# Small inputs first on another queue, a split first load, and two stores on the loads' queue in a rotary-embedding kernel

## The chip, the cores and the metric

One core of one Trainium2 chip. The metric is the device time of one execution in microseconds (us); a profile's span is about 1.8 us shorter, since it runs only from the first to the last instruction. All runs compared here are of the fast state, unless it is said otherwise. Most runs of a kernel lie within 0.3% of its median. A transfer is "asked for" when an engine issues it and "lands" when its semaphore reports the whole of it. Units, casts and stores are counted from 0 in the order of work, loads X1 to X7 by their unit.

## The reference, cut to what matters

```python
# x: (8, 8, 1024, 64) fp32, 16.78 MB; freqs: 32 fp32; positions: 1024 integers
angles = np.outer(positions * scale, freqs)
cos, sin = np.cos(angles), np.sin(angles)
x_first, x_second = x[..., :half], x[..., half:]
out_first  = x_first * cos - x_second * sin
out_second = x_first * sin + x_second * cos
```

All of x is read once and all of the output, as large, is written once. The sine and cosine tables depend on positions and freqs alone and are the same for every head.

## The kernel before

x is cut into eight units of 2 MiB (128 partitions, 16 KiB each). Unit 0 comes as fp32 from SyncE and is cast by ScalarE. Units 1 to 7 are cast to fp16 by the transfer itself, issued from GpSimd. VectorE does four fp16 passes a unit, 6.93 us in all; ScalarE casts the result into one of four fp32 OUT buffers, which is stored from SyncE. The first of the four passes writes the tile ps. Before the first unit stands the table chain: positions and freqs, two small matmuls, four passes on VectorE, two sines on ScalarE.

```python
BUF_O = 4
...
    X0f = xin.tile([P, N], FP32, name="X0f")
    nc.sync.dma_start(out=X0f, in_=xv[0])

    pos_i64 = consts.tile([HP, K], positions.dtype)
    nc.scalar.dma_start(out=pos_i64, in_=positions.rearrange("(q k) -> q k", k=K))
    freq_row = consts.tile([1, half], FP32)
    nc.scalar.dma_start(out=freq_row, in_=freqs[None, :])
    ...
    load(1)                    # nc.gpsimd.dma_start(X[1], fp32 -> fp16)
    ...                        # two GpSimd instructions build sel
    for u in range(2, NU):
        load(u)
    ...                        # tables: cfreq, pos_ps, y, m, r, sinT, ra, cosT
    for u in (1, 0, *range(2, NU)):
        ps = prods.tile([P, K, 2, half], FP16, tag="ps")
        ...                    # four VectorE instructions on X[u] and ps
        OUT = xout.tile([P, N], FP32, tag="O")
        pin(nc.scalar.copy(out=OUT, in_=X[u].rearrange("p k h j -> p (k h j)")))
        nc.sync.dma_start(out=ov[u], in_=OUT)
```

Of the kernel before, what the change touches and what calls it, by code (L numbers as in the profile page):

```python
# [1 line left out]

# [1 line left out]

# [4 lines left out]

FP32 = mybir.dt.float32
FP16 = mybir.dt.float16
I32 = mybir.dt.int32
AF = mybir.ActivationFunctionType
ALU = mybir.AluOpType

_MAGIC = 12582912.0
_TWO_PI_DN = float(np.float32(np.uint32(0x40C90FDA).view(np.float32)))

BUF_O = 4  # L20
BUF_P = 2


@with_exitstack
def kernel(
    ctx: ExitStack,
    tc: tile.TileContext,
    x: bass.AP,
    freqs: bass.AP,
    positions: bass.AP,  # L30
    scale: bass.AP,
    out: bass.AP,
):
    nc = tc.nc

    B, Hh, S, D = x.shape
    NBH = B * Hh
    half = D // 2
    P = nc.NUM_PARTITIONS
    HEADS = 8  # L40
    HP = P // HEADS
    K = S // HP
    N = K * D
    NU = NBH // HEADS
    assert S % HP == 0 and D == 2 * half and NBH % HEADS == 0

    fscale = float(scale)

    xv = x.rearrange("b h s d -> (b h s d)").rearrange("(u p n) -> u p n", p=P, n=N)
    ov = out.rearrange("b h s d -> (b h s d)").rearrange("(u p n) -> u p n", p=P, n=N)  # L50

    consts = ctx.enter_context(tc.tile_pool(name="consts", bufs=1))
    tmp = ctx.enter_context(tc.tile_pool(name="tmp", bufs=1))
    psum = ctx.enter_context(tc.tile_pool(name="psum", bufs=1, space=bass.MemoryType.PSUM))
    xin = ctx.enter_context(tc.tile_pool(name="xin", bufs=1))
    xout = ctx.enter_context(tc.tile_pool(name="xout", bufs=BUF_O))
    prods = ctx.enter_context(tc.tile_pool(name="prods", bufs=BUF_P))


    X0f = xin.tile([P, N], FP32, name="X0f")  # L60
    nc.sync.dma_start(out=X0f, in_=xv[0])

    pos_i64 = consts.tile([HP, K], positions.dtype)
    nc.scalar.dma_start(out=pos_i64, in_=positions.rearrange("(q k) -> q k", k=K))  # L64
    freq_row = consts.tile([1, half], FP32)
    nc.scalar.dma_start(out=freq_row, in_=freqs[None, :])

    X = [xin.tile([P, K, 2, half], FP16, name=f"X{u}") for u in range(NU)]

    def load(u):  # L70
        nc.gpsimd.dma_start(out=X[u].rearrange("p k h j -> p (k h j)"), in_=xv[u])  # L71


    sel = consts.tile([HP, HEADS, HP], FP32)
    load(1)
    nc.gpsimd.memset(sel, 0.0)
    nc.gpsimd.affine_select(  # L77
        out=sel, in_=sel, compare_op=ALU.not_equal, fill=1.0, base=0,
        pattern=[[0, HEADS], [-1, HP]], channel_multiplier=1,
    )  # L80
    for u in range(2, NU):
        load(u)

    pin = tc.keep_in_program_order


    coef = consts.tile([1, P], FP32)
    pin(nc.vector.memset(coef, fscale / (2.0 * np.pi)))  # L88
    quarter = consts.tile([P, 1], FP32)
    pin(nc.vector.memset(quarter, np.pi / 2.0))  # L90
    cfreq = psum.tile([P, half], FP32)
    nc.tensor.matmul(out=cfreq, lhsT=coef, rhs=freq_row, start=True, stop=True)  # L92

    pos_row = consts.tile([HP, K], FP32)
    pin(nc.vector.tensor_copy(  # L95
        out=pos_row,
        in_=pos_i64.bitcast(I32).rearrange("p (k t) -> p k t", t=2)[:, :, 0],
    ))
    pos_ps = psum.tile([P, K], FP32)
    nc.tensor.matmul(  # L100
        out=pos_ps, lhsT=sel.rearrange("q a b -> q (a b)"), rhs=pos_row, start=True, stop=True
    )
    posf = consts.tile([P, K], FP32)
    pin(nc.vector.tensor_copy(out=posf, in_=pos_ps))  # L104

    y = tmp.tile([P, K, half], FP32)
    pin(nc.vector.tensor_tensor(  # L107
        out=y,
        in0=posf.unsqueeze(2).broadcast_to((P, K, half)),
        in1=cfreq.unsqueeze(1).broadcast_to((P, K, half)),  # L110
        op=ALU.mult,
    ))
    m = tmp.tile([P, K, half], FP32)
    pin(nc.vector.tensor_scalar(out=m, in0=y, scalar1=_MAGIC, scalar2=None, op0=ALU.add))  # L114
    r = tmp.tile([P, K, half], FP32)
    pin(nc.vector.scalar_tensor_tensor(  # L116
        out=r, in0=m, scalar=_MAGIC, in1=y, op0=ALU.subtract, op1=ALU.subtract
    ))
    sinT = consts.tile([P, K, half], FP16)
    pin(nc.scalar.activation(out=sinT, in_=r, func=AF.Sin, bias=0.0, scale=-_TWO_PI_DN))  # L120
    ra = tmp.tile([P, K, half], FP32)
    pin(nc.vector.tensor_scalar(  # L122
        out=ra.bitcast(I32), in0=r.bitcast(I32), scalar1=0x7FFFFFFF, scalar2=None, op0=ALU.bitwise_and
    ))
    cosT = consts.tile([P, K, half], FP16)
    pin(nc.scalar.activation(out=cosT, in_=ra, func=AF.Sin, bias=quarter, scale=-_TWO_PI_DN))  # L126
    pin(nc.scalar.copy(out=X[0].rearrange("p k h j -> p (k h j)"), in_=X0f))  # L127

    cos_b = cosT.unsqueeze(2).broadcast_to((P, K, 2, half))
    sin_b = sinT.unsqueeze(2).broadcast_to((P, K, 2, half))  # L130


    for u in (1, 0, *range(2, NU)):
        ps = prods.tile([P, K, 2, half], FP16, tag="ps")
        pin(nc.vector.tensor_tensor(out=ps, in0=X[u], in1=sin_b, op=ALU.mult))  # L135
        pin(nc.vector.tensor_tensor(out=X[u], in0=X[u], in1=cos_b, op=ALU.mult))  # L136
        pin(nc.vector.tensor_tensor(  # L137
            out=X[u][:, :, 0, :], in0=X[u][:, :, 0, :], in1=ps[:, :, 1, :], op=ALU.subtract
        ))
        pin(nc.vector.tensor_tensor(  # L140
            out=X[u][:, :, 1, :], in0=ps[:, :, 0, :], in1=X[u][:, :, 1, :], op=ALU.add
        ))
        OUT = xout.tile([P, N], FP32, tag="O")
        pin(nc.scalar.copy(out=OUT, in_=X[u].rearrange("p k h j -> p (k h j)")))  # L144
        nc.sync.dma_start(out=ov[u], in_=OUT)


# [1 line left out]
_INS = ['x', 'freqs', 'positions', 'scale']  # L149
_OUTS = [((8, 8, 1024, 64), 'float32')]  # L150

_NUMBERS = {'scale': 0.5}


# [26 lines left out]
```

## Time and profile before

| | before |
|---|---|
| median time, 3 runs | 85.48 us (85.28 to 85.62) |
| span | 83.9 us |
| VectorE busy | 62.6 us, from 9 to 73 with no gap over 0.7 us |
| DMA engines | full from about 4 us to 82 us |
| bytes | 16.79 MB read, 16.78 MB written |

The prediction below shows the main lines. Two more views matter for what came of it. The first is the page's list of transfers: what, from which queue, KB each, us from issue to landing.

```profile
X0f<-in_x_dram SPq DMA_DIRECT2D x1, 2048.0 KB, 10.2
pos_i<-in_positions_dram ACTq DMA_DIRECT2D x1, 8.0 KB, 4.1
```

Positions, 8 KB, are 4.1 us on the way beside unit 0. The second is the table by stretches at the end; its last two columns are the busy share of the DMA engines and the GB/s moved.

```profile
76.00:77.00 1.00, 0.00 (x0) 0.00 (x0) 0.00 (x0) 0.41 (x1) 0.00 (x0) 1.00 0.62 262
```

Just as the last store is asked for (76.43), the DMA engines have a small dent. They had almost run out of stores at the moment when the last one came. By the semaphore record of the trace it landed at 82.68, 6.25 us after it was asked for. The experiments below show that this is what a store takes with no other store ahead of it.

### The profile page before, as it was taken

The numbers are of one execution on the slowest core, as the hardware profiler recorded it, in microseconds if no ns is written. First come the engines' busy times: TensorE is split into PE (matmuls) and PEld (weight loads), VectorE is DVE, ScalarE is ACT, GpSimd is POOL, SyncE is SP. The second block draws the span as 40 slices with busy tenths as digits, with TensorE's granted clock in tenths as the row PEclk, the third lists the DMA queues.
The fourth block names the chain that finished last, engine by engine and source line by source line (L and its number), as shares of the span: only waits on it lengthen the run. The fifth ranks groups of instructions, "written<-read, shape, count | busy, mean of one in ns | idle before, by whom it ended". The sixth has DMA issues, their size and how long they took to land.

```text
span 83.9 us, 151 instructions
## 1 busy us (share of the span) xinstructions
PE 1.1 (1%) x4; PEld 0.9 (1%) x4; DVE 62.6 (75%) x40; ACT 37.4 (45%) x12; POOL 4.5 (5%) x13
## 2 busy tenths in 40 slices
PE   0002300000000000000000000000000000000000
PEld 0002200000000000000000000000000000000000
DVE  0010699889999999999999999999999999600000
ACT  1400000799749309608905921950880591294000
POOL 5960000000000000000000000000000000000000
DMA  3599999999999999999999999999999999998890
GB/s 78 207 402 328 289 207 219 215 211 223 203 230 203 231 191 238 313 336 305 313 348 324 313 313 277 426 438 438 438 430 414 445 414 430 438 430 375 375 500 0
DMA packets 2338, 26.22 MB, mean 313 GB/s; under 512 B 274, under 2 KB 290, under 8 KB 290
## 3 DMA queue, kind: packets, MB, share of 16 engines
q1 hardware_dynamic: 1296, 18.87, 53.6%
q0 software_dynamic: 1008, 7.34, 42.7%
q10 hardware_dynamic: 34, 0.01, 0.2%
HBM read 16.79 MB, written 16.78 MB: 400 GB/s over the span
## 4 chain that ended last, share of the span: by engine, by line
DVE 72%; DMA 8%; ACT 7%; DVEq 1%; PE 1%; issue 1%; ACTq 1%
DVE X L136 22%; DVE ps L135 21%; DVE X L137 12%; DVE X L140 9%; DMA freq_row<-in_freqs_dram 8%; ACT OUT L144 4%; DVE r L116 3%; DVE y L107 3%; ACT sinT L120 2%; DVE m L114 1%; DVEq L176 1%; PE cfreq L92 1%; PE pos_ps L100 1%; ACTq L64 0%; DVE posf L104 0%
## 5 line engine op out<-in xcount | busy, mean ns | idle before, releaser
L144 ACT CAST OUT<-X 128x4096 f32<-128x4096 f16 x8 | 28.8, 3605 | 25.0 <-DVE X L140 25.0
L135 DVE TENSOR_TENSOR ps<-X,sinT 128x4096 f16<-128x4096 f16 x8 | 18.3, 2284 | 0.7 <-ACT sinT L120 0.7
L136 DVE TENSOR_TENSOR X<-X,cosT 128x4096 f16<-128x4096 f16 x8 | 18.3, 2292 | 0.3
L137 DVE TENSOR_TENSOR X<-X,ps 128x2048 f16<-128x2048 f16 x8 | 9.8, 1224 | 0.3
L140 DVE TENSOR_TENSOR X<-ps,X 128x2048 f16<-128x2048 f16 x8 | 9.7, 1217 | 0.0
L120 ACT ACTIVATE sinT<-r 128x2048 f16<-128x2048 f32 x1 | 1.9, 1910 | 12.2 <-DVE r L116 12.2
L71 POOL DMA_DIRECT2D X<-in_x_dram x7 | 3.9, 567 | 0.8 <-POOLq L162 0.8
L127 ACT CAST X<-X0f 128x4096 f16<-128x4096 f32 x1 | 3.6, 3587 | 0.0
L104 DVE COPY posf<-pos_ps 128x64 f32<-128x64 f32 x1 | 0.2, 225 | 4.0 <-PE pos_ps L100 4.0
L95 DVE CAST pos_row<-pos_i 16x64 f32<-16x64 int32 x1 | 0.2, 241 | 3.9 <-DMA pos_i<-in_positions_dram 3.9
L116 DVE SCALAR_TENSOR_TENSOR r<-m,y 128x2048 f32<-128x2048 f32 x1 | 2.3, 2292 | 0.0
L107 DVE TENSOR_TENSOR y<-posf,cfreq 128x2048 f32<-128x2048 f32 x1 | 2.3, 2286 | 0.0
L120 ACT ACT_TABLE_LOAD x1 | 1.3, 1283 | 1.7 <-issue 1.7
L126 ACT ACTIVATE cosT<-ra,quarter 128x2048 f16<-128x2048 f32 x1 | 2.0, 1985 | 0.0
L114 DVE TENSOR_SCALAR m<-y 128x2048 f32<-128x2048 f32 x1 | 1.2, 1227 | 0.0
L122 DVE TENSOR_SCALAR ra<-r 128x2048 int32<-128x2048 int32 x1 | 1.2, 1226 | 0.0
L88 DVE MEMSET coef<- 1x128 f32 x1 | 0.2, 165 | 0.8 <-PEq L162 0.8
L92 PE MATMUL cfreq<-freq_row,coef 1*128 1x32 f32 x2 | 0.6, 392 | 8.0 <-DMA freq_row<-in_freqs_dram 8.0
L100 PE MATMUL pos_ps<-pos_row,sel 16*128 16x64 f32 x2 | 0.7, 432 | 0.0
L92 PEld LDWEIGHTS cfreq<-freq_row,coef 1*128 1x128 f32 x2 | 0.5, 308 | 7.9 <-issue 7.9
L100 PEld LDWEIGHTS pos_ps<-pos_row,sel 16*128 16x128 f32 x2 | 0.5, 328 | 0.0
L77 POOL TENSOR_SCALAR_AFFINE_SELECT sel<-sel 16x128 f32<-16x128 f32 x1 | 0.3, 332 | 0.1
(6 smaller groups left out, 0.7 us busy)
## 6 DMA issues: line engine op xcount, KB each, us to landing
out_dram<-OUT SPq DMA_DIRECT2D x8, 2048.0 KB, 14.3
X<-in_x_dram POOLq DMA_DIRECT2D x7, 1024.0 KB, 24.5
X0f<-in_x_dram SPq DMA_DIRECT2D x1, 2048.0 KB, 10.2
pos_i<-in_positions_dram ACTq DMA_DIRECT2D x1, 8.0 KB, 4.1
freq_row<-in_freqs_dram ACTq DMA_DIRECT2D x1, 0.1 KB
```

Source lines behind the costliest of these rows:

```text
L71: nc.gpsimd.dma_start(out=X[u].rearrange("p k h j -> p (k h j)"), in_=xv[u])
L100: nc.tensor.matmul(out=pos_ps, lhsT=sel.rearrange("q a b -> q (a b)"), rhs=pos_row, start=True, stop=True)
L107: pin(nc.vector.tensor_tensor(out=y, in0=posf.unsqueeze(2).broadcast_to((P, K, half)), in1=cfreq.unsqueeze(1).broadcast_to((P, K, half)), ...
L114: pin(nc.vector.tensor_scalar(out=m, in0=y, scalar1=_MAGIC, scalar2=None, op0=ALU.add))
L116: pin(nc.vector.scalar_tensor_tensor(out=r, in0=m, scalar=_MAGIC, in1=y, op0=ALU.subtract, op1=ALU.subtract))
L120: pin(nc.scalar.activation(out=sinT, in_=r, func=AF.Sin, bias=0.0, scale=-_TWO_PI_DN))
L127: pin(nc.scalar.copy(out=X[0].rearrange("p k h j -> p (k h j)"), in_=X0f))
L135: pin(nc.vector.tensor_tensor(out=ps, in0=X[u], in1=sin_b, op=ALU.mult))
L136: pin(nc.vector.tensor_tensor(out=X[u], in0=X[u], in1=cos_b, op=ALU.mult))
L137: pin(nc.vector.tensor_tensor(out=X[u][:, :, 0, :], in0=X[u][:, :, 0, :], in1=ps[:, :, 1, :], op=ALU.subtract))
L140: pin(nc.vector.tensor_tensor(out=X[u][:, :, 1, :], in0=ps[:, :, 0, :], in1=X[u][:, :, 1, :], op=ALU.add))
L144: pin(nc.scalar.copy(out=OUT, in_=X[u].rearrange("p k h j -> p (k h j)")))
```

## The change

The intent, as the diff reads: let the two small inputs go first on a queue of their own beside two half loads of unit 0, and keep the first two stores out of the loads' way by putting them behind the loads on GpSimd's queue.

```diff
-    nc.sync.dma_start(out=X0f, in_=xv[0])
+    nc.sync.dma_start(out=X0f[:, : N // 2], in_=xv[0][:, : N // 2])
+    nc.scalar.dma_start(out=X0f[:, N // 2 :], in_=xv[0][:, N // 2 :])
...
-    nc.scalar.dma_start(out=pos_i64, in_=positions.rearrange("(q k) -> q k", k=K))
+    nc.gpsimd.dma_start(out=pos_i64, in_=positions.rearrange("(q k) -> q k", k=K))
...
-    nc.scalar.dma_start(out=freq_row, in_=freqs[None, :])
+    nc.gpsimd.dma_start(out=freq_row, in_=freqs[None, :])
...
-    for u in (1, 0, *range(2, NU)):
+    for i, u in enumerate((1, 0, *range(2, NU))):
...
-        nc.sync.dma_start(out=ov[u], in_=OUT)
+        (nc.gpsimd if i < 2 else nc.sync).dma_start(out=ov[u], in_=OUT)
```

## The prediction

> **What bounds the kernel now.** I began with the page's busy shares and slices.
>
> ```profile
> PE 1.1 (1%) x4; PEld 0.9 (1%) x4; DVE 62.6 (75%) x40; ACT 37.4 (45%) x12; POOL 4.5 (5%) x13
> ...
> DVE  0010699889999999999999999999999999600000
> ...
> DMA  3599999999999999999999999999999999998890
> ```
>
> Two rows are full: VectorE from 9 to 73 us, and the DMA engines from about 4 us to the end. The chain of work that ended last follows VectorE only:
>
> ```profile
> 1.19 6.64 DMA freq_row<-in_freqs_dram
> 7.82 0.14 issue
> 7.96 0.60 PE cfreq L92 x2
> ...
> 15.24 1.92 ACT sinT L120
> 17.16 0.02 issue
> 17.19 2.30 DVE ps L135
> ```
>
> Read alone, it promises that each microsecond taken from the arrival of freq_row (7.82) is a microsecond off the end. The chain stops, however, at the last cast (72.80 + 3.60 = 76.4) and does not show the transfers after it. So I asked for the time to landing of every load and store alone, by windows around its issue. Issue plus landing gives: X0f 11.0; X1 to X7 at 13.4, 18.2, 23.1, 28.0, 34.5, 44.3, 54.1; stores 0 to 7 at 42.8, 52.6, 58.2, 63.0, 67.8, 72.7, 77.6 and 82.5 (the last from SyncE's final wait of 5.1 us that begins at 76.8). Here is the answer for the store issued at 69.5:
>
> ```profile
> DMA to landing us min/median/max: 8.1/8.1/8.1
> ```
>
> What matters is the spacing. Loads alone land every 4.85 us (13.4, 18.2, 23.1, 28.0). Stores alone land every 4.87 us (63.0 to 82.5). VectorE makes a unit only every 6.93 us. A store issued every 6.93 us that lands every 4.87 us has been working off a queue, and that queue lasts to the end: store 7 is issued at 76.4, while store 6 lands at 77.6. The DMA table by stretches agrees:
>
> ```profile
> 20.00:24.00 4.00, 0.00 (x0) 0.00 (x0) 3.97 (x3) 2.54 (x1) 0.00 (x0) 1.00 1.07 223
> ...
> 60.00:68.00 8.00, 0.00 (x0) 0.00 (x0) 7.93 (x5) 4.68 (x2) 0.00 (x0) 1.00 1.00 430
> ```
>
> The last columns are DMA share and GB/s. Loads cast to 16 bits are counted by bytes written, so 223 is about 446 GB/s read. All sixteen units (8 in, 8 out, 2 MiB each at the fp32 side) at 4.86 us are 77.8 us of transfer, in a span of 83.9. My reading: the chain and the DMA engines end within about 1 us of one another, and both must shrink for a gain.
>
> **What the Trainium skill says.** (1) "DMA: Bandwidth & Descriptors", section "Issuing engines are not separate DMA queues": transfers from SyncE, ScalarE and GpSimd run on the same 16 engines and interleave, so another issuer saves only issue time. The trace agrees: with loads on one queue and stores on the other, X6, X7 and store 1 land 9.8 us after their predecessors (34.5, 44.3, 54.1; 42.8, 52.6), twice 4.87. (2) Same page, "Queues, rings and completion order": each engine takes the queues in turn, a packet at a time, in order within one queue. That fits freq_row, a few bytes, taking 6.64 us behind positions on ScalarE's queue beside two bulk streams, and it says where the moved stores go: behind all loads on GpSimd's queue. (3) "SBUF — State Buffer", section "SBUF: two separate sides": GpSimd cannot write descriptors while VectorE runs an instruction in a two-port mode. The moved stores are issued while VectorE runs tensor_tensor at the usual rates; the trace before has no GpSimd issue in that stretch, so no number here tests it.
>
> **The change, part by part.**
>
> *Small inputs.* Removed: two issues on ScalarE (0.41 and 0.53 us). Added: two at the head of GpSimd's list, about 0.55 us each by the load issues there (median 557 ns), so 1.2 to 2.3 us; every load issue and the sel selection (now 2.65 to 2.98, then about 3.8 to 4.1) move back by 1.1. Freq_row no longer has a 16 KiB load packet of its own queue or of X1 before it; each turn it waits for a half row (8 KiB) from each of two queues. Before, positions landed at 4.84 and freq_row 3.0 us later. With turns about half as long and a start at about 2.3 I estimate positions at 4.0 and freq_row at 5.0 (4.5 to 6). The first ps then starts at 5.0 + 9.4 (7.82 to 17.19 in the chain) = 14.4, if X1 is there. Shift of the VectorE chain: 2.8 us.
>
> *Unit 0 in halves.* The same bytes. The first 3 us move little (147 and 115 GB/s in the stretches 1 to 2 and 2 to 3), about 1.3 us of engine time lost; two queues may fill some of it, while X1 asked for 1.1 us later and two small transfers with completion writes on all engines may add some. I call the net d = 0, between -0.7 and +0.6. X0f and X1 together are two units whatever their order, so X1 lands at 13.4 + d, before 14.4.
>
> *First two stores behind the loads.* Stores 0 and 1 (issued about 25.3 and 32.2) cannot start until X7 is in. The loads then run alone at 4.85: X7 at 13.4 + 6 x 4.85 = 42.5 instead of 54.1. VectorE gets nothing from it: it wanted X7 at 65.7. But mixed traffic stops. From 33.7 to 53.3[...] before moved 2 loads and 1.82 stores, 5.13 us a unit against 4.86, so the mix cost 3.82 x 0.27 = 1.0 us. After, all eight stores are done at best at 42.5 + 8 x 4.87 = 81.5 + d, against 82.5.
>
> *The price: four OUT buffers.* Cast 4 reuses the buffer of store 0, cast 5 that of store 1. Store 2 goes from SyncE at 41.8 - 2.8 = 39.0; in before the first store took some 3.4 us to get its share beside loads (X5 came at 34.5, not 32.9), so it starts about when the loads end. Then stores 0 and 2 share: both land at 42.5 + 9.7 = 52.2. Cast 4 was at 52.04 and would be ready at 49.2; it waits 3 us, ends at 55.8. Stores 1 and 3 share and land at 61.9; cast 5, ready at 56.2, waits to 61.9 and ends at 65.6. Store 4, alone from 61.9, lands at 66.8, so store 5, issued at 65.7, is just in time. ScalarE then has 3.6 us a cast against VectorE's 6.93: cast 6 ends 69.3, cast 7 (ready at 70.0) 73.6, store 7 is asked for at 73.7 and the queue is still three units deep. So the stall costs nothing if store 4 is whole at 61.9; if a fraction a of it is already done, the DMA engines idle 4.87a. I allow 0.4 us in the mean.
>
> *Sum.* 82.5 -> 81.5 + 0.4 + d = 81.9, that is -0.6 us, with the chain's 2.8 us unused. Rounding with d perhaps slightly in favour: 85.48 - 0.7 = 84.8.
>
> **The rivals.**
> R1, the chain is the only bound: the end follows freq_row, -2.8 us, 82.7. For: the chain view, and VectorE without a gap from 17 to 73. Against: the landings show the store queue just emptying when store 7 arrives; a store 7 asked for at 73.6 would find 1.0 unit more ahead of it. It would need the mixing and starting losses to go as well.
> R2, the buffers bite: if SyncE's stores get more than half of the turns, stores 0 and 1 land later, casts 4 and 5 wait longer and the DMA engines run dry for 1 to 3 us: 86 to 88. For: four buffers, and only about 1 us of slack at store 5. Against: loads and stores shared evenly in before.
> R3, nothing changes: freq_row lands no earlier behind GpSimd's slower path, and the end stays at 85.5.
> Mine, R0: the DMA engines become the sole bound; a gain below 1 us.
>
> **Range and chances.** R0 with d and a gives 84.0 to 85.8. R1 in part pulls down to 83.4, R2 up past 86. Range 83.4 to 86.3. The 2% lines are 83.8 and 87.2. Faster 0.18 (d strongly negative, or mixing worth more than 1 us), slower 0.06 (R2 in full), within 0.76.
>
> **What would show it.** Right: the first ps at 14 to 15; X7 landed by 44; loads every 4.85 us; stores 0 and 1 landing near 52 and 62 and ScalarE's casts 4 and 5 waiting for them, not for VectorE, 3 and 6 us; VectorE ended by 71; the DMA share about full to the last store, which lands 81 to 82.5, some 8 us after its issue instead of 6. Wrong: a last store landing within 6 us of its issue (R1), a hole in the DMA row near 60 to 70 (R2), freq_row still near 7.8 (R3), or X7 landing much before 42, which would say that the start was worth more than I allow.

## The result, and the profile after

| | before | after |
|---|---|---|
| median time, 4 runs each | 85.38 us | 86.22 us (86.16 to 86.52) |
| ratio | | 1.0106 (95%: 1.0066 to 1.0146) |
| positions land | 4.8 | 7.5 |
| freq_row lands | 7.8 | 8.7 |
| first ps starts | 17.19 | 18.10 |
| X1 / X7 land | 13.4 / 54.1 | 13.5 / 43.1 |
| store 6 lands | 77.6 | 77.2 |
| store 7 asked for | 76.43 | 77.34 |
| store 7 lands | 82.7 | 83.6 |

A ratio here and below is the mean time of one kernel's fast runs over that of the kernel before in the same rounds, so not quite the ratio of the medians. The change is 1.1% slower: inside the predicted range and within 2%, but on the other side of zero from the point given (84.8).

The chain of work that ended last, after the change:

```profile
1.28 0.61 POOL pos_i L65
1.90 6.83 DMA freq_row<-in_freqs_dram
8.73 0.14 issue
8.87 0.60 PE cfreq L93 x2
...
16.15 1.92 ACT sinT L121
18.07 0.02 issue
18.10 2.30 DVE ps L136
```

Freq_row lands at 8.73 instead of 7.82. From there to the first ps the path takes 9.37 us in both kernels, so the whole of VectorE's work starts 0.91 us later. The list of transfers after:

```profile
X0f<-in_x_dram ACTq DMA_DIRECT2D x1, 1024.0 KB, 8.4
X0f<-in_x_dram SPq DMA_DIRECT2D x1, 1024.0 KB, 8.2
pos_i<-in_positions_dram POOLq DMA_DIRECT2D x1, 8.0 KB, 6.2
freq_row<-in_freqs_dram POOLq DMA_DIRECT2D x1, 0.1 KB, 6.8
```

The halves were asked for at 0.74 and 0.75 and land at 9.1 and 8.9; positions, asked for at 1.28, land at 7.5. Where that time went is seen in the table of DMA queues (packets, MB, share of the engines). In the stretch from 1 to 5.7 us it lists the queues of SyncE (q1) and ScalarE (q10) alone:

```profile
q1 hardware_dynamic: 80, 0.66, 46.9%
q10 hardware_dynamic: 75, 0.61, 33.5%
```

From 5.7 to 8.3 it has GpSimd's queue too:

```profile
q0 software_dynamic: 83, 0.16, 30.6%
```

Narrower stretches place the single packets. The first packet of positions moves at 5.73, 4.45 us after they were asked for, when 155 of the 256 packets of unit 0 have started. From then on they do go between the packets of the bulk: positions' data from 5.73, their completion from 6.36, freq_row's data from 6.98 and its completion from 7.54, each some 0.6 us after the one before, which is the time of two bulk packets of 8 KiB (0.31 us each in the trace). So the small inputs are late because their first turn is late. The other end of the kernel, in the page's row of DMA shares in 40 slices and in the table by stretches:

```profile
DMA  3799999999999999999999999999999999990982
```

```profile
76.00:77.00 1.00, 0.00 (x0) 0.00 (x0) 0.00 (x0) 1.00 (x1) 0.00 (x0) 1.00 0.09 33
77.00:78.00 1.00, 0.00 (x0) 0.00 (x0) 0.00 (x0) 0.31 (x1) 0.00 (x0) 1.00 0.00 0
```

The row has a 0 in slice 37. For almost 2 us the DMA engines have nothing to do: ScalarE is still casting the last unit (the 1.00 and 0.31 in the fourth busy column). And the time to landing of store 6, by itself, which was 8.1 us before:

```profile
DMA to landing us min/median/max: 6.8/6.8/6.8
```

Of these 1.3 us, 0.91 is only that store 6 was asked for later (70.42 instead of 69.51); it landed 0.4 us earlier, at 77.17. That gain was thrown away waiting for store 7, which comes 0.91 us later than before because the tables were 0.91 us later. It then lands 6.3 us after it was asked for, at 83.6.

### The profile page after: what moved, and what is told of

Read it like the earlier page. It is cut to its first block, busy times and chain, and to the rows that moved or that the text cites. A ratio compares the mean times of both kernels' runs of the same rounds, so it can differ in the third digit from the quotient of the medians.

```text
span 84.5 us, 153 instructions
## 1 busy us (share of the span) xinstructions
PE 1.1 (1%) x4; PEld 0.9 (1%) x4; DVE 62.5 (74%) x40; ACT 37.4 (44%) x12; POOL 6.6 (8%) x17
## 4 chain that ended last, share of the span: by engine, by line
DVE 71%; DMA 8%; ACT 7%; issue 2%; DVEq 1%; PE 1%; POOL 1%; ACTq 0%; POOLq 0%
DVE X L137 22%; DVE ps L136 21%; DVE X L138 12%; DVE X L141 9%; DMA freq_row<-in_freqs_dram 8%; ACT OUT L145 4%; DVE r L117 3%; DVE y L108 3%; ACT sinT L121 2%; DVE m L115 1%; DVEq L177 1%; POOL pos_i L65 1%; PE cfreq L93 1%; PE pos_ps L101 1%; DVE posf L105 0%
## 5 line engine op out<-in xcount | busy, mean ns | idle before, releaser
L146 POOL DMA_DIRECT2D out_dram<-OUT x2 | 1.1, 534 | 27.3 <-ACT OUT L145 27.3
L65 POOL DMA_DIRECT2D pos_i<-in_positions_dram x1 | 0.6, 618 | 0.8 <-POOLq L163 0.8
```

## The experiments

Theory T: two bounds lie within 1 us of each other. One is the chain: store 7 cannot land before it is asked for plus 6.3 us. The other is transfer: the DMA engines need 4.87 us for each of 16 units. The change made the chain longer, since the small inputs were asked for after 2 MiB of bulk, and made the transfers shorter, by putting loads and stores apart; the longer of the two counts. Rivals: the moved stores cost the time (U); GpSimd's transfers are slow in themselves (S); two bulk queues crowd out a third (H); only the chain counts (R1).

### 1 and 2. Each part alone

loads_only takes the changed kernel and sends all stores from SyncE:

```diff
-        (nc.gpsimd if i < 2 else nc.sync).dma_start(out=ov[u], in_=OUT)
+        nc.sync.dma_start(out=ov[u], in_=OUT)
```

> The load part alone (halves from SyncE and ScalarE, positions and freqs on GpSimd), all stores from SyncE as before. Theory T (positions and freqs are late because the bulk halves were asked for 0.5 and 1.2 us ahead of them): positions near 7.5 us, freqs near 8.7, first ps at 18.1 as in the changed kernel, store 7 asked for at 77.3. Loads and stores mix again, so store 6 lands near 77.6 to 78 and store 7 near 82.9 to 83.4: time 85.8 to 86.3. Rival U (the moved stores cost the time): freqs and time go back to 85.4, the kernel before.

stores_only takes the kernel before and has only the reverse of this edit.

> The store part alone on the kernel before. Theory T: freqs at 7.8, store 7 asked for at 76.4; X7 lands near 42.5 to 43, the store queue is empty about 1 us before store 7 is asked for, store 7 lands 6.3 us after that at 82.7: 85.3 to 85.7, the same as before, since the saved DMA time becomes a hole in the DMA row at 75 to 77. Rival U: 86.2, as the changed kernel.

Measured: loads_only 86.59 us, ratio 1.0136 (1.0114 to 1.0159); freq_row at 8.4, store 7 asked for at 77.0. stores_only 85.47 us, ratio 1.0003 (0.9988 to 1.0018). The time of loads_only is 0.3 us above what T expected; all the loss is in the load part, and U is out. In stores_only X7 lands at 42.9 and store 6 at 77.0, 0.5 us earlier than before (0.3 of it was there when X1 landed, at 13.15 instead of 13.43), and this is where that went:

```profile
76.00:77.00 1.00, 0.00 (x0) 0.00 (x0) 0.00 (x0) 0.13 (x1) 0.00 (x0) 1.00 0.08 33
```

The dent of the kernel before (share 0.62) has become a hole (0.08). The end stays with store 7, asked for at 76.2. Cast 5 did wait 4.8 us for store 1 to free its buffer there, and it cost nothing.

### 3. Why positions and freqs come late

bulk_behind_small keeps both first on GpSimd, at the same issue times, and moves unit 0 behind X1:

```diff
-    nc.sync.dma_start(out=X0f[:, : N // 2], in_=xv[0][:, : N // 2])
-    nc.scalar.dma_start(out=X0f[:, N // 2 :], in_=xv[0][:, N // 2 :])
...
     load(1)
+    nc.gpsimd.dma_start(out=X0f, in_=xv[0])
```

> The changed kernel, but unit 0 is asked for whole from GpSimd behind X1, so no bulk bytes are ahead of positions and freqs, which still go first on GpSimd. Theory Q (they are late because 2 MiB of unit 0 was asked for before them): positions land at 3 to 4, freqs at 3.5 to 5, although the issuing engine and both issue times stay. Rival S (GpSimd's transfers are slow in themselves): positions near 7.5 and freqs near 8.7 again. The time matters less here: 85 to 87, with casts 4 and 5 waiting for buffers.

whole_small_gp only puts unit 0 back into one load from SyncE.

> The changed kernel with unit 0 whole from SyncE again (one bulk queue, not two), positions and freqs still first on GpSimd. Theory Q: the same 2 MiB are ahead, so positions near 7, freqs near 8.4, time 86.0 to 86.4. Rival H (two bulk queues take two turns of three and crowd GpSimd's queue out): with one, positions land by 4.5 to 5 and freqs by 6, time 85.2 to 85.6.

The lists of transfers, bulk_behind_small first:

```profile
pos_i<-in_positions_dram POOLq DMA_DIRECT2D x1, 8.0 KB, 1.8
freq_row<-in_freqs_dram POOLq DMA_DIRECT2D x1, 0.1 KB, 1.7
```

```profile
X0f<-in_x_dram SPq DMA_DIRECT2D x1, 2048.0 KB, 7.7
pos_i<-in_positions_dram POOLq DMA_DIRECT2D x1, 8.0 KB, 6.2
freq_row<-in_freqs_dram POOLq DMA_DIRECT2D x1, 0.1 KB, 6.5
```

From the same engine and at the same time, the two take 1.8 and 1.7 us with no bulk ahead of them, and 6.2 and 6.5 with one bulk load ahead. S is out, since the issuing engine is the same. H is out, since one bulk queue does what two do (86.1 us, ratio 1.0076, 1.006 to 1.0093). The bulk asked for half a microsecond earlier is the cause; small_first_hw below, where bulk is asked for on two queues 0.4 us after the small inputs, agrees (1.7 us for positions). By the packets, what grows is the wait for the first turn: with no bulk ahead positions' first packet moved at 2.58, 1.3 us after they were asked for; behind unit 0 it moved at 5.39 in whole_small_gp, when 77 of its 128 rows had started, and at 5.73 in the changed kernel. X1 of the kernel before, asked for 0.5 us after unit 0, also starts only at 5.70, after 79 of 128. Why the first turn comes so late was not tested. bulk_behind_small was itself slow, 87.0 us (1.0185): with unit 0 asked for late, X1 and X0f were both in at 15.2 instead of 13.4, and casts 4 and 5 waited 16.1 us in all for buffers.

### 4 and 5. An early table chain

small_first_hw asks for positions first on SyncE and freqs first on ScalarE, each ahead of its half of unit 0; small_first_hw_sp_stores has all stores on SyncE as well.

```diff
-    nc.gpsimd.dma_start(out=pos_i64, in_=positions.rearrange("(q k) -> q k", k=K))
-    nc.gpsimd.dma_start(out=freq_row, in_=freqs[None, :])
+    nc.sync.dma_start(out=pos_i64, in_=positions.rearrange("(q k) -> q k", k=K))
+    nc.scalar.dma_start(out=freq_row, in_=freqs[None, :])
+    # then the two halves of X0f from SyncE and ScalarE, as in the change
```

> The changed kernel with positions asked for first on SyncE and freqs first on ScalarE, each ahead of its half of unit 0; stores 0 and 1 still from GpSimd. Theory T: both land by 2.5 to 4 us; the first ps then waits for X1 at 13.4 or starts near 13; store 7 asked for 72.5 to 74. The DMA engines are the bound: X7 near 43, then eight stores at 4.87 = 82 at best, casts 4 and 5 wait for buffers; time 84.6 to 86. Rival R1 (chain only): the end moves with the chain, 4 to 5 us earlier than the changed kernel, 81.5 to 82.5.

> The same with all stores from SyncE. Theory T: early chain as there; loads and stores mixed at 5.1 us a unit for some 20 us; last store lands 82 to 83, time 85 to 86, about 0.5 to 1 us above the kernel with stores behind the loads unless the buffers' wait costs that one more. Rival R1: 81.5 to 82.5, equal to it.

Both small inputs were in by 2.5 us. With all stores on SyncE the first ps started at 14.27 and store 7 was asked for at 73.51, 2.9 us earlier than in the kernel before. The time: 85.61 us, ratio 1.0019 (1.0004 to 1.0033). Nothing came of 2.9 us, and R1 (81.5 to 82.5) is out. The stretch of its table after store 7 was asked for:

```profile
74.00:76.00 2.00, 0.00 (x0) 0.00 (x0) 0.00 (x0) 0.00 (x0) 0.00 (x0) 1.00 1.05 451
```

All engines are done and the DMA engines are full; store 7 lands 9.4 us after it was asked for, at 82.9. This is the other bound.

small_first_hw, with stores 0 and 1 behind the loads, was 87.04 us, ratio 1.0196 (1.0144 to 1.0248), outside what T expected (84.6 to 86). The waits and the stretches of small_first_hw say why:

```profile
ACT OUT L144 <- DMA out_dram<-OUT: 15.6, 2, 9.4
```

```profile
66.00:68.00 2.00, 0.00 (x0) 0.00 (x0) 1.97 (x2) 2.00 (x1) 0.00 (x0) 1.00 0.41 172
68.00:70.00 2.00, 0.00 (x0) 0.00 (x0) 1.47 (x2) 2.00 (x2) 0.00 (x0) 1.00 0.61 262
```

Store 0 landed at 54.7 and store 1 at 64.5. Casts 4 and 5, ready long before on VectorE's side, stood 9.4 and 6.2 us waiting for those two buffers; ScalarE then made three casts in a row (2.00 of 2.00), and meanwhile the DMA engines ran dry at a share of 0.41 and 0.61.

### 6. The same with six OUT buffers

small_first_hw_o6 makes room by computing in place and uses X0f, which is free by then, as a sixth buffer:

```diff
-BUF_O = 4
+BUF_O = 5
-    r = tmp.tile([P, K, half], FP32)
+    r = y
-    ra = tmp.tile([P, K, half], FP32)
+    ra = m
-        OUT = xout.tile([P, N], FP32, tag="O")
+        OUT = X0f if i == 5 else xout.tile([P, N], FP32, tag="O")
```

> small_first_hw with six OUT buffers (five, and X0f's space once it is free; r and ra are written over y and m to make room), so no cast waits for stores 0 and 1. If the buffers made small_first_hw slow: casts wait for VectorE only, no hole in the DMA row, the last store lands at 13.9 + 6 x 4.86 + 8 x 4.87 = 82.0 instead of 84.4, time 84.7 to 85.4. If the two queues of stores are slow in themselves: near 87 again.

Measured: 85.75 us, ratio 1.0032 (1.0016 to 1.0049), so the buffers were about 1.3 us of small_first_hw. No cast waits for a transfer, and the hole is gone:

```profile
66.00:70.00 4.00, 0.00 (x0) 0.00 (x0) 3.43 (x3) 0.68 (x2) 0.00 (x0) 1.00 1.03 442
```

Even so it does not beat the kernel before, and it missed its forecast (84.7 to 85.4). Unit 0 was asked for 0.45 us later, behind the small inputs, and X1 came at 13.8 instead of 13.4; that such a late start is carried to the end of the transfer bound is argued, not tested.

### 7 to 9. Candidates that failed

swap_o6 is stores_only with six buffers and freqs ahead of positions on ScalarE.

> Candidate: the kernel before with freqs ahead of positions on ScalarE's queue, unit 0 whole from SyncE, stores 0 and 1 from GpSimd, six OUT buffers. Theory: freqs at 2 to 2.5, positions near 5 instead of freqs at 7.8, so the chain is 2.5 us earlier and the DMA engines never run dry; X1 at 13.3, the last store at 13.3 + 29.2 + 39.0 = 81.5: 84.4 to 84.9, 0.6 to 1.2% faster than before. If only the chain counted: 82.9.

Freq_row then landed at 2.1, but positions, now second (asked for at 1.27), at 7.9: the wait only changed its name. Its first packet moved at 5.50, when 77 of the 128 rows of unit 0 had started. 85.73 us, against 84.4 to 84.9 expected, ratio 1.0031 (1.0019 to 1.0043).

quarter_o6 is swap_o6 with a quarter of unit 0 asked for at the start, and the rest after positions.

```diff
-    nc.sync.dma_start(out=X0f, in_=xv[0])
+    nc.sync.dma_start(out=X0f[:, : N // 4], in_=xv[0][:, : N // 4])
     # on ScalarE: freqs, then positions, then
+    nc.scalar.dma_start(out=X0f[:, N // 4 :], in_=xv[0][:, N // 4 :])
```

> Candidate: SyncE asks for only a quarter of unit 0 (0.5 MiB) at the start; ScalarE asks for freqs, then positions, then the other three quarters. Stores 0 and 1 from GpSimd, six OUT buffers. Theory Q (what counts for a small transfer is the bulk asked for before it): freqs at 2.1, positions at 3 to 4.5 although second on ScalarE's queue (7.9 where the whole of unit 0 was ahead), and bulk bytes flow from the start, so X1 lands at 13.4. The chain is then 3 us early, no cast waits for a buffer, the DMA engines never run dry: last store at 13.4 + 29.2 + 39.0 = 81.6, time 84.4 to 85.0 (0.6 to 1.2% faster than before). If positions are late again (7.8), the last store is asked for at 76.3 and the time is 85.5.

> The same with four OUT buffers. Theory: casts 4 and 5 wait for stores 0 and 1, 4 and 9 us, store 5 is late and the DMA row has a hole near 65 to 70; 85.8 to 87. If the buffers do not matter: as quarter_o6.

Positions, again second on ScalarE's queue, landed at 5.4, when the quarter did (5.2): with a quarter of the bulk ahead the wait is 4.1 us instead of 6.6. But the start was slow, and this candidate lost on it: 86.5 us, against 84.4 to 85.0 expected, ratio 1.0146 (1.0114 to 1.0177). Its table between 3 and 5 us:

```profile
3.00:4.00 1.00, 0.00 (x0) 0.00 (x0) 0.00 (x0) 0.40 (x1) 1.00 (x3) 1.00 1.12 188
4.00:5.00 1.00, 0.00 (x0) 0.00 (x0) 0.00 (x0) 0.00 (x0) 1.00 (x3) 1.00 0.89 197
```

The engines count as busy, yet move 188 and 197 GB/s, where the kernel before moves 393 between 4 and 6. Part of that is the count: X1 already flows here, and its bytes are counted as written, half of those read. Counted as read it is about 260 against 410. X1 lands at 15.2 and X0f at 15.5. Whether the rows of 4 and 12 KiB or the three queues at once are to blame was not separated. VectorE's first ps still started 1.9 us earlier than in the kernel before, and the last store landed 0.9 us later (83.5): once more the transfers decide. quarter_o4 gave 88.23 us, but three of its four runs, the profiled one among them, count as slow, and the fast one (86.32) has no profile; it says nothing about the buffers.

### 10 and 11. Closing the hole at the end

If the changed kernel waits only for store 7, it must gain when part of store 7 is asked for earlier. after_split_tail changes only the last unit:

```diff
+        if i == NU - 1:
+            for lo in (0, N // 2):
+                pin(nc.scalar.copy(out=OUT[:, lo : lo + N // 2], in_=Xf[:, lo : lo + N // 2]))
+                nc.sync.dma_start(out=ov[u][:, lo : lo + N // 2], in_=OUT[:, lo : lo + N // 2])
+            continue
```

> The changed kernel with the last unit's cast and store in two halves of columns. In the changed kernel the DMA engines stand idle from 76.2 to 78.0 waiting for store 7. Theory (the end of the changed kernel is set by when store 7 is asked for, not by transfer): the first half is asked for at 75.6, the hole closes to under 0.5 us, the last half lands near 82.1 to 82.4 instead of 83.6: time 84.7 to 85.3, 1.0 to 1.6 us below the changed kernel. Rival (the transfers set it): 86.2 as before the split.

> Candidate: the kernel before, stores 0 and 1 from GpSimd, the last cast and store in halves. Six-store landing there is 77.0; with the hole closed the last half lands at 77.0 + 4.9 = 81.9 instead of 82.5: time 84.7 to 85.0, 0.5 to 0.9% faster than before.

after_split_tail: 85.08 us, ratio 0.9976 (0.9961 to 0.9991), where the changed kernel stood at 1.0106. The same two stretches as above:

```profile
76.00:77.00 1.00, 0.00 (x0) 0.00 (x0) 0.00 (x0) 1.00 (x1) 0.00 (x0) 1.00 0.65 270
77.00:78.00 1.00, 0.00 (x0) 0.00 (x0) 0.00 (x0) 0.40 (x1) 0.00 (x0) 1.00 0.96 401
```

Shares 0.65 and 0.96 in place of 0.09 and 0.00; the last half was asked for at 77.4, no earlier than store 7 was, and landed at 82.0 instead of 83.6. The late tables are all still there (first ps as late as in the changed kernel), and 1.1 us of time are gone. So it was the hole. stores_split_tail, which has the stores' part and the split but not the loads' part, is the lowest of all: 84.99 us, ratio 0.9952 (0.9935 to 0.9969), half a per cent below the kernel before; its lead over after_split_tail (85.08 in the same rounds) is within the noise. Its profiled run was its slowest (85.92; the others 84.82 to 85.15), so its trace is not used here.

## Why the prediction was right or wrong

- **The two bounds: right.** "The chain and the DMA engines end within about 1 us of one another, and both must shrink for a gain." Experiment 5 gained 2.9 us on the chain and nothing on the time; experiment 2 gained 0.5 us of transfer and nothing on the time. But the prediction put the end before at 82.5, on the store queue. Store 7 landed at 82.68, 6.25 us after it was asked for, as it did where the queue stood empty (6.26 in loads_only, 6.27 in stores_only and in the changed kernel). One more spacing after store 6 would have given 77.56 + 4.87 = 82.43. So the chain already set the end, by about 0.25 us.
- **Small inputs: wrong, and this is the step that failed.** "I estimate positions at 4.0 and freq_row at 5.0", from "a start at about 2.3" and "each turn it waits for a half row (8 KiB) from each of two queues". Measured: 7.5 and 8.7. The turns were right: from their first packet positions took 1.75 us and freq_row 3.0, against the 1.7 and 2.7 that the estimate allows from its start. The start was wrong: the first packet moved at 5.73, not at 2.3. The trace before had the evidence. Positions, asked for together with unit 0, moved from 2.87 and took 4.1 us; freq_row, asked for 0.45 us later, had its one packet at 6.25 and took 6.64; X1, asked for at 1.23, first moved at 5.70. The prediction read freq_row's 6.64 us as turns. Rival R3 named the late arrival, but for a reason (GpSimd's path) that experiment 3 refutes.
- **So "the DMA engines become the sole bound": wrong.** With the chain 0.91 us later instead of 2.8 earlier, the chain became the bound by a wide margin (the transfers alone would have let store 7 land at 77.17 + 4.87 = 82.0, it landed at 83.6), and the sum came out at +0.8 us instead of -0.7.
- **Unit 0 in halves: right.** X1 was put at 13.4 + d with d near 0; it came at 13.5.
- **Stores behind the loads: right for X7, not for the gain.** X7 was put at 42.5 and came at 43.1. Of the 1.0 us that mixing was said to cost, 0.4 showed at store 6. The 5.13 us a unit rest on a wrong count. From 33.53 to 53.12, where the last packets of X5 and X7 end, the DMA table before lists both queues:

```profile
q0 software_dynamic: 288, 2.10, 51.1%
q1 hardware_dynamic: 288, 4.19, 51.1%
```

That is two loads (2.10 MB as written) and 2.00 stores, not 1.82: 4.90 us a unit, hardly more than apart. (These two times stand in place of the 33.7 and 53.3 of the prediction, which it got by taking 0.8 us off the landings of X5 and X7.)

- **The price of four buffers: right in kind, but it needed the early chain.** The waits of 3 and 6 us at casts 4 and 5 did not appear in the changed kernel: there store 1 landed at 59.0 and cast 5 was ready at 59.86. With the chain early (small_first_hw) they appeared, larger than thought for cast 4 (9.4 and 6.2 us): X7 came at 45.0 since store 2 already shared the engines with the last load, and stores 0 and 1 at 54.7 and 64.5 instead of 52.2 and 61.9. Store 4 landed 3.6 us after store 1 and not 4.87, so about a quarter of it was done by then: the fraction a of the prediction. It allowed 0.4 us for it; experiment 6 puts it near 1.3.
- **Rival R1: wrong as a forecast of a gain, right as to which side decides.** The end did follow freq_row, only freq_row went the other way.
- **Its signs.** X7 by 44 came true. The first ps at 14 to 15 (18.1), the waits at casts 4 and 5, VectorE done by 71 (73.6) and a last store some 8 us after its issue (6.3) did not; freq_row stayed near its old place (8.7), the sign of R3.
- **Slips that changed nothing.** A store 7 asked for at 73.6 finds 2.8 / 4.87 = 0.6 of a unit more ahead of it, not 1.0; and by the prediction's own 81.5 the queue at 73.7 is 1.6 units deep, not three.
- **Issuing from GpSimd under VectorE: no block seen.** The trace after has the number that the prediction missed: the two stores issued from GpSimd under tensor_tensor took 534 ns each to issue, the loads issued from it 549. "SBUF — State Buffer", section "Who interferes with whom", has no two-port mode for tensor_tensor, and this agrees.

## What to carry to other kernels

When two bounds end together, a change that shortens one and lengthens the other shows only the longer; look at the last transfer (when it was asked for, how long after that it landed) to see which one it is, and split the last piece of work if the transfers stand idle waiting for it. A few bytes that start a long chain arrive early only if they are asked for before any bulk transfer, on whatever of the three queues; half a microsecond late cost 4.4 to 4.9 us here. It pays only as far as the chain is the bound: asked for first, they gained 2.9 us of chain and no time (85.61 us). Before putting stores behind loads, count the buffers that those stores hold.

## What the Trainium skill lacked or had wrong

- "DMA: Bandwidth & Descriptors", section "Queues, rings and completion order", says that each engine takes its queues in turn at packet granularity. That fits loads beside stores (9.8 us apart, twice 4.87), and the small inputs once they move (0.6 us a turn). What it lacks is when the first turn comes: 8 KB on a queue of its own, asked for 0.5 us after 2 MiB on one or two other queues, first moved after 4.1 to 4.45 us, when about 60% of the bulk had started, against 1.3 us with no bulk ahead. What holds it so long was not found.
- The same page, section "Issuing engines are not separate DMA queues", was borne out: one or two issuing queues for unit 0 made no gain (86.1 and 86.22 us). But it says that another issuer saves only issue time. The choice of issuer also sets the order, which that section does not say: two stores put on the loads' queue moved X7 from 54.1 to 42.9. (It follows from the order within a queue in the section above, and the prediction took it from there.)
- No page was found that gives the cost of mixing loads and stores. These runs show little of it: 4.90 us a unit of 2 MiB mixed (before, 33.53 to 53.12), against 4.85 for loads alone (X1 to X4). From X1 to store 6 it is 0.2 us in stores_only against before and 0.6 in the changed kernel against loads_only, but small_first_hw_sp_stores, mixed, is as quick (63.9 us) as stores_only.
